# Fifteen small loads into an unread tile, issued behind the last row load of a sum of reciprocals

## The chip, the cores and the metric

The kernel runs on one core of a Trainium2 chip. The metric is device time in microseconds (us). A profile of one execution is at hand: its span runs from the first to the last instruction. In it PE is the matrix engine (PEld its weight loads), DVE the vector engine, ACT the activation engine, POOL the general engine, and SP the engine that issues all of this kernel's DMAs (SPq is its instruction queue).

## The reference

The input x is 32 x 512 x 1024 in float32, all positive. Each row of 1024 numbers gives one result, the sum of its reciprocals:

```python
def reference(x: np.ndarray) -> np.ndarray:
    return np.sum(1.0 / x, axis=-1).astype(np.float32)
```

## The kernel before

The 16384 rows are laid out as 128 partitions by F = 128 rows, so that a "row" of the kernel is 128 x 1024 numbers, 512 KB. A row is cut into two halves a and b. Because 1/a + 1/b = (a + b) / (a b), the kernel forms the product of the halves (POOL at L199, or DVE at L220 after PE has copied one half to PSUM at L209), takes its reciprocal on ACT as exp(-ln(.)) (L242 and L251), forms the sum of the halves on PE as two accumulating matmuls with the identity (L232) for some rows, and lets DVE multiply and sum along the row (L267) into one column of the tile `sums`. The last two rows, 126 and 127, are cut into two parts each, of 256 KB; so there are F + 2 = 130 work items.

The order of everything is written out by hand in the string PLAN (L38 to L73). Each token is an operation, an item number and perhaps a count and a bank: D loads the next so many items, P and V or W make products, C and S are matmuls, L and E the two activations, R the final reduction. The loop at L179 walks through the plan and issues the operations; each engine's queue keeps that order.

All DMAs are issued by SP, in this order:

- Loads (L187), into the tile `ring` of R = 40 row slots, so a later load must wait until the row that had its slot before has been used. There are 33 load instructions. The last four load 256 KB each: items 126 to 129. We number them load 1 to load 33.
- Six stores of finished columns of `sums` (L289), 19 columns each, which are put out when the first DONE = 114 rows have been reduced. We call them stores 1 to 6.
- One last store of the remaining 14 columns (L291), after the whole plan. We call it store 7.

The framework gives each DMA one of a small set of completion semaphores in turn, and puts the waits into the issuing queue. In the trace of this kernel, SP has one separate wait instruction at L187 for each of 25 of the 33 loads, and from load 9 on a DMA is issued only after the DMA eight places earlier has landed. So SP's queue is a chain with a stride of eight DMAs: load 33 behind load 25, store 1 behind load 26, and so on, besides the waits on compute engines. The function `note` (L135) records who touches which piece of the ring, a product slot or a bank, and declares some of the implied waits unnecessary. The direct stores at L289 and L291 are not passed to it.

After the body comes the end of the program (L317): SP waits for all DMAs, and the engines meet at barriers.

Of the kernel before, what the change touches and what calls it, by code (L numbers as in the profile page):

```python
# [11 lines left out]
def kernel(  # L12
# [5 lines left out]
    nc = tc.nc  # L18
    f32 = mybir.dt.float32
# [3 lines left out]
    F = 128  # L23
# [56 lines left out]
    x_v = x.flatten_outer_dims().rearrange("(p f) d -> p f d", p=P)  # L80
# [12 lines left out]
    pool = ctx.enter_context(tc.tile_pool(name="pool", bufs=1))  # L93
# [4 lines left out]
    prod = pool.tile([P, NP, H], f32)  # L98
    sums = pool.tile([P, F], f32)
    ident = pool.tile([P, P], f32)  # L100
    ps = pspool.tile([P, 8, H], f32)
    make_identity(nc, ident)

# [15 lines left out]
    def xs(r, h):  # L119
        q, at, w = place(r)  # L120
        return ring[:, q % R, at + h * w : at + (h + 1) * w]

    loaded = 0
# [54 lines left out]
    with tc.manual_schedule():  # L178
        for op, r, n, b in ops:  # L179
            p = pslot.get(r)  # L180
            if op == "D":
                n, r = r, loaded
                while n:
# [4 lines left out]
                        out=ring[:, a : a + m, at : at + 2 * w],  # L188
                        in_=x_v[:, q : q + m, at : at + 2 * w],
                    )  # L190
                    note("SP", inst, writes=rows(r, m))
                    r, n = r + m, n - m
                loaded = r
            elif op == "P":
                while n:
                    q, at, w = place(r)
# [3 lines left out]
                        out=prod[:, p : p + m, :w],  # L200
# [16 lines left out]
            elif op in "WV":  # L217
# [3 lines left out]
                    out=prod[:, p, :w], in0=xs(r, 0), in1=in1, op=mult  # L221
# [35 lines left out]
            elif op == "R":  # L257
# [4 lines left out]
                else:  # L262
# [5 lines left out]
                    out=row,  # L268
# [53 lines left out]
```

## Time and profile before

| what | value |
|---|---|
| time, median of 2 runs (168.21 and 168.22) | 168.22 us |
| span of the profiled execution | 166.3 us |
| granted PE clock, mean | 0.990 |
| PE busy | 132.5 us, 80% |
| DVE busy | 128.3 us, 77% |
| ACT busy | 132.3 us, 80% |
| POOL busy | 128.2 us, 77% |
| HBM read over the span | 67.11 MB, 404 GB/s |
| last load (load 33) issued | 153.51 us |
| store 7 issued | 164.06 us |

The profiled execution has no separate time on record; its span is 1.9 us less than the median of the runs, which is what lies before its first and after its last instruction. Every time of day below is counted from the start of that span. DMA issue is not counted as busy time in the profile, so SP does not appear among the engines of the first part; its instructions are found in the timeline and in the waits of SP.

### The profile page before, as it was taken

The numbers are of one execution on the slowest core, as the hardware profiler recorded it, in microseconds if no ns is written. First come the engines' busy times: TensorE is split into PE (matmuls) and PEld (weight loads), VectorE is DVE, ScalarE is ACT, GpSimd is POOL, SyncE is SP. The second block draws the span as 40 slices with busy tenths as digits, with TensorE's granted clock in tenths as the row PEclk, the third lists the DMA queues.
The fourth block names the chain that finished last, engine by engine and source line by source line (L and its number), as shares of the span: only waits on it lengthen the run. The fifth ranks groups of instructions, "written<-read, shape, count | busy, mean of one in ns | idle before, by whom it ended". The sixth has DMA issues, their size and how long they took to land.

```text
span 166.3 us, 1348 instructions
## 1 busy us (share of the span) xinstructions
PE 132.5 (80%) x292; PEld 55.2 (33%) x292; DVE 128.3 (77%) x282; ACT 132.3 (80%) x157; POOL 128.2 (77%) x81
## 2 busy tenths in 40 slices
PE   0000799978855999999999999988699979989982
PEld 0000333333312444444343433324234424433351
DVE  0000119885787699898998898989899999999994
ACT  3040073949995899999799999996999999999992
POOL 1500795069995999999999999948977869999860
PEclk9999999999996999999999999999999999999999
DMA  5999999999998989999999999999999999999940
GB/s 189 536 394 394 441 441 441 441 441 441 441 441 349 509 368 446 430 417 438 441 434 434 406 426 446 429 424 424 414 437 437 414 410 428 410 409 410 400 139 4
DMA packets 5768, 67.26 MB, mean 404 GB/s; under 512 B 1536, under 2 KB 1536, under 8 KB 3200
## 3 DMA queue, kind: packets, MB, share of 16 engines
q1 hardware_dynamic: 5760, 67.18, 95.6%
q8 instruction: 2, 0.03, 0.1%
q14 instruction: 6, 0.05, 0.1%
HBM read 67.11 MB, written 0.07 MB: 404 GB/s over the span
## 4 chain that ended last, share of the span: by engine, by line
DMA 57%; PE 18%; ACT 8%; DVE 6%; POOL 6%; issue 3%; SPq 1%; ACTq 0%; POOLq 0%; DVEq 0%
DMA ring<-in_x_dram 57%; PE ps L232 15%; POOL prod L199 6%; ACT prod L242 4%; PE ps L209 3%; ACT ps L251 2%; DVE ring L267 2%; DVE prod L267 2%; ACT prod L251 2%; DVE prod L220 1%; SPq L187 1%; DVE sums L267 0%; ACTq L242 0%; POOLq L199 0%; DVEq L317 0%
## 5 line engine op out<-in xcount | busy, mean ns | idle before, releaser
L199 POOL TENSOR_TENSOR prod<-ring 128x1024 f32<-128x1024 f32 (+2 forms) x75 | 127.5, 1727 | 33.5 <-DMA ring<-in_x_dram 27.1
L232 PE MATMUL ps<-ring,ident 128*128 128x512 f32 (+1 forms) x260 | 116.9, 596 | 5.2 <-DVE sums L267 4.5
L242 ACT ACTIVATE prod<-prod 128x1024 f32<-128x1024 f32 (+2 forms) x78 | 68.5, 892 | 24.9 <-DVE prod L220 14.3
L267 DVE CUSTOM_DVE_ANT_1 ring<-ring,ps 128x1024 f32<-128x1024 f32 (+1 forms) x65 | 76.4, 1208 | 8.9 <-ACT ps L251 8.7
L232 PEld LDWEIGHTS ps<-ring,ident 128*128 128x128 f32 x260 | 49.2, 193 | 71.7 <-issue 51.6
L267 DVE CUSTOM_DVE_ANT_0 prod<-prod,ps 128x512 f32<-128x512 f32 (+1 forms) x63 | 40.9, 677 | 0.4 <-PE ps L232 0.4
L209 PE MATMUL ps<-ring,ident 128*128 128x512 f32 x32 | 19.3, 689 | 25.7 <-DMA ring<-in_x_dram 24.0
L251 ACT ACTIVATE ps<-prod 128x1024 f32<-128x1024 f32 (+2 forms) x41 | 34.1, 838 | 4.5 <-DVE sums L267 3.7
L251 ACT ACTIVATE prod<-prod 128x1024 f32<-128x1024 f32 (+3 forms) x37 | 34.4, 931 | 0.9
L220 DVE TENSOR_TENSOR prod<-ring,ps 128x512 f32<-128x512 f32 x16 | 10.9, 684 | 26.3 <-PE ps L209 26.3
L209 PEld LDWEIGHTS ps<-ring,ident 128*128 128x128 f32 x32 | 6.0, 213 | 36.0 <-issue 21.4
L267 DVE DVE_READ_ACCUMULATOR2_ANT sums<- 128x1 f32 x130 | 10.7, 82 | 0.0
L220 DVE TENSOR_TENSOR prod<-ring 128x512 f32<-128x512 f32 x6 | 4.1, 688 | 0.1
L84 ACT ACT_TABLE_LOAD x1 | 1.3, 1283 | 0.7 <-PEq L306 0.7
L267 DVE CUSTOM_DVE_ANT_0 prod<-prod,ps,sums 128x256 f32<-128x256 f32 x2 | 0.9, 475 | 0.0
masks.py:197 POOL MEMSET ident<- 128x128 f32 x1 | 0.2, 204 | 0.3 <-POOLq L306 0.3
masks.py:199 POOL TENSOR_SCALAR_AFFINE_SELECT ident<-ident 128x128 f32<-128x128 f32 x1 | 0.3, 292 | 0.1
L306 POOL MEMSET const-float32-0.0<- 128x1 f32 x1 | 0.1, 98 | 0.2 <-issue 0.2
L306 POOL MEMSET const-bfloat16-1.0<- 128x1 bf16 x1 | 0.1, 101 | 0.0
L306 POOL MEMSET const-uint8-127<- 128x1 uint8 x1 | 0.1, 101 | 0.0
L306 POOL MEMSET const-float32-1.0<- 128x1 f32 x1 | 0.1, 98 | 0.0
## 6 DMA issues: line engine op xcount, KB each, us to landing
ring<-in_x_dram SPq DMA_DIRECT2D x2, 7168.0 KB, 41.2
ring<-in_x_dram SPq DMA_DIRECT2D x2, 3584.0 KB, 29.3
ring<-in_x_dram SPq DMA_DIRECT2D x2, 3072.0 KB, 31.9
ring<-in_x_dram SPq DMA_DIRECT2D x3, 2048.0 KB, 34.0
ring<-in_x_dram SPq DMA_DIRECT2D x1, 5632.0 KB, 30.3
ring<-in_x_dram SPq DMA_DIRECT2D x5, 1024.0 KB, 31.8
ring<-in_x_dram SPq DMA_DIRECT2D x1, 5120.0 KB, 16.5
ring<-in_x_dram SPq DMA_DIRECT2D x1, 4608.0 KB, 30.7
```

The lines of the kernel that those rows point to most:

```text
L84: nc.scalar.add_instruction(mybir.InstLoadActFuncSet(name=nc.get_next_instruction_name(), act_func_set_id=act_sets.index("natural_log_exp_ ...
L187: inst = nc.sync.dma_start(out=ring[:, a : a + m, at : at + 2 * w], in_=x_v[:, q : q + m, at : at + 2 * w],)
L199: inst = nc.gpsimd.tensor_tensor(out=prod[:, p : p + m, :w], in0=ring[:, a : a + m, at : at + w], in1=ring[:, a : a + m, at + w : at + 2 * w],
L209: inst = nc.tensor.matmul(ps[:, b, : place(r)[2]], lhsT=ident, rhs=xs(r, 1), start=True, stop=True,)
L220: inst = nc.vector.tensor_tensor(out=prod[:, p, :w], in0=xs(r, 0), in1=in1, op=mult)
L232: inst = nc.tensor.matmul(ps[:, b, : place(r)[2]], lhsT=ident, rhs=xs(r, h), start=h == 0, stop=h == 1,)
L242: inst = nc.scalar.activation(out=pg, in_=pg, func=Ln, scale=S)
L251: inst = nc.scalar.activation(out=rc, in_=pg, func=Exp, scale=-1.0)
L267: inst = nc.vector.tensor_tensor_reduce(out=row, in0=row, in1=other, scale=S, scalar=total if q in summed else 0.0, op0=mult, op1=add, acc ...
L306: nc = _bacc.Bacc("TRN2", target_bir_lowering=False, num_devices=1)
```

## The change

One more tile, `few`, of 16 x 136 float32 numbers is allocated after the others. When the last load has been issued, fifteen more loads follow it on SP: number k takes k + 1 numbers of each of k partitions from the input's first row into the columns of `few` that begin at k(k+1)/2. The column ranges of the fifteen don't overlap, each moves 4k(k+1) bytes (8 to 960), and nothing reads `few`. All else stays. In the queue of SP they stand behind load 33 and ahead of store 1. We call them tiny 1 to tiny 15.

```diff
     ident = pool.tile([P, P], f32)
+    few = pool.tile([16, 136], f32)
     ps = pspool.tile([P, 8, H], f32)
...
                 loaded = r
+                if loaded == F + 2:
+                    for k in range(1, 16):
+                        c = k * (k + 1) // 2
+                        nc.sync.dma_start(
+                            out=few[:k, c : c + k + 1], in_=x_v[:k, 0, c : c + k + 1]
+                        )
             elif op == "P":
```

## Prediction

> **What bounds the kernel now.** I read the page first, then the chain that ended last, then the waits of SP and SP's issues in the last 25 us, because the change touches only SP's queue.
>
> The page shows a kernel that is balanced on four engines and on DMA. Its strip of DMA use says when the loads stop:
>
> ```profile
> PE 132.5 (80%) x292; PEld 55.2 (33%) x292; DVE 128.3 (77%) x282; ACT 132.3 (80%) x157; POOL 128.2 (77%) x81
> DMA  5999999999998989999999999999999999999940
> ```
>
> The reader is to see that DMA is full until the slice that begins near 158 us (slices are 4.16 us) and free after 162: 4.4 us remain in which small transfers meet no traffic.
>
> The end of the chain of waits (start, us, what):
>
> ```profile
> 162.88 0.09 DVE prod L267
> 162.97 0.17 issue
> 163.14 0.08 DVE sums L267
> 163.23 0.18 DVE prod L267
> 163.40 0.14 issue
> 163.54 0.08 DVE sums L267
> 163.63 0.39 DVE prod L267
> 164.02 0.01 DVEq L317
> ```
>
> DVE sets the end: its last sum is ready at 164.03 and store 7 goes out at 164.06. The waits of SP over the whole span (who waited for whom: us in total, times, longest):
>
> ```profile
> SPq L187 <- DMA ring<-in_x_dram: 42.6, 16, 5.7
> SPq L289 <- DMA ring<-in_x_dram: 4.2, 6, 1.0
> SPq L291 <- DVE sums L267: 3.5, 1, 3.5
> SPq L291 <- DMA ring<-in_x_dram: 0.2, 1, 0.2
> ```
>
> All six stores wait for a load, though they read nothing that it writes: this is the stride of eight. The fourth line is the same for store 7, and the third is SP's slack: it stands idle 3.5 us until DVE is done. The issues of SP, from narrow windows of its timeline:
>
> ```profile
> 153.51 0.33 SPq L187 DMA_DIRECT2D ring<-in_x_dram  x1
> 154.80 0.35 SPq L289 DMA_DIRECT2D out_dram<-sums  x1
> 159.97 0.33 SPq L289 DMA_DIRECT2D out_dram<-sums  x1
> 164.06 0.33 SPq L291 DMA_DIRECT2D out_dram<-sums  x1
> ```
>
> Between them stores 2 to 5 went out at 156.08, 157.36, 158.69 and 159.36. The time from issue to landing, from the DMA view of the windows that hold loads 26 (issued 142.18), 33 and store 7, last column:
>
> ```profile
> ring<-in_x_dram SPq DMA_DIRECT2D x1, 512.0 KB, 12.6
> ring<-in_x_dram SPq DMA_DIRECT2D x1, 256.0 KB, 7.8
> out_dram<-sums SPq DMA_DIRECT2D x1, 7.0 KB, 1.4
> ```
>
> Load 26 lands at 142.18 + 12.6 = 154.78 and store 1 goes out at 154.80. Loads 27 to 32 land, by the same sum, at 156.07, 157.38, 158.69, 159.33, 159.86 and 160.54, and stores 2 to 6 follow them. Load 33 lands at 153.51 + 7.8 = 161.31.
>
> **The change part by part.** Nothing is removed. The unread tile costs no instruction. Fifteen DMA issues are put into SP's queue; what is queued behind them is stores 1 to 7 and SP's end of program, and no compute engine waits for those. Loads 1 to 33 stand ahead, so the compute chain up to 164.03 keeps its times. The bytes (4k(k+1) each, 5.4 KB in all) are nothing beside 67 MB, and stand behind the loads.
>
> 1. Tiny 1 to 7 take the places of the stores in the stride of eight: they wait for loads 26 to 32 and go out at 154.80, 156.08, 157.36, 158.69, 159.36, 159.97 and about 160.57. Cost nothing: the loads' landings 0.5 to 1.3 us apart cover an issue of about 0.4. Without that cover it would be an issue each, 7 x 0.4 = 2.8 us.
>
> 2. Tiny 8 waits for load 33: 161.31, issued about 161.33. Here the slack goes: where SP used to stand idle from 160.6, it now has 8 tiny and 6 stores ahead of store 7.
>
> 3. Tiny 9 to 15 wait for tiny 1 to 7. Store 1, issued at the same 154.80, landed 6.7 us later, at 161.5, as soon as the loads ahead of it were through; tiny 1 should be through by then too, so this costs at most 0.1 us, and the rest are bound by SP's own issue time. That price for a DMA of 1 to 15 partitions is not in the trace: all of its 40 have 128 partitions. Nearest rows: 29 isolated loads take 0.327 to 0.33, the first four, back to back, begin at 0.74, 1.17, 1.64 and 2.11, so 0.43 to 0.47 apart; the fourth takes 0.80 itself. From issue to issue that is 0.33 + 0.05 = 0.38 (the gap between the first loads is 0.05) at the low end, 0.43 to 0.47 in the back-to-back rows, and 0.85 at the worst. Nothing says that a small DMA must be dearer or cheaper to issue. I take 0.425, the middle between the isolated and the dearest normal row, since these are back to back but have few pieces: 8 x 0.425 = 3.40, so store 1 goes out at 161.33 + 3.40 = 164.73.
>
> 4. Stores 1 to 6: six issues at 0.38 (the row 0.332 to 0.348 and the gap) = 2.28, and about 0.05 for each of three separate semaphore waits, which stand ahead of stores 5 to 7 (17 ns and a gap each) = 0.15. Their landing waits are old: store 1 needs tiny 8, issued 3.4 us before, where store 7 landed after 1.4 and store 6, behind loads, after 2.4. Store 7 goes out at 164.73 + 2.28 + 0.15 = 167.16 instead of 164.06.
>
> 5. After store 7 all stays: 1.4 us to landing, then the barriers to 166.31. By then stores 1 to 6 would land at their own 1.4 after issue, ahead of store 7.
>
> Sum: 167.16 - 164.06 = 3.10 us, so a span of 169.4. The profiled span of 166.3 stands 1.9 under the median of 168.22, and that part isn't touched: 168.22 + 3.10 = **171.3 us**, 1.8% more.
>
> Ends of the unknown: at 0.327 for each of the 14 issues, with no gap, 161.33 + 4.58 + 0.15 = 166.06, 2.0 us more, 170.2. At 0.70 per tiny, toward the dear row of 0.80, 161.33 + 5.60 + 2.43 = 169.36, 5.3 us more, 173.5. At 0.85, tiny 5 to 8 would slip too (159.36 + 3 x 0.85 = 161.91), and store 7 would go out at 171.1, 7.1 us more: 175.3.
>
> Against the middle price stands a rule of the Trainium skill, page "DMA: Bandwidth & Descriptors", section "Why a DMA increments its semaphore by 16 and not by 1": a transfer is spread over the largest number of engines up to 16 that divides its outermost size, and where that is below 16 the issuing sequencer itself writes the missing part of the semaphore count. All the tiny loads are such, and no row here shows one; the page gives no price for it on this chip. By it alone the issue would be dearer than 0.38, and each 0.1 us more would add 0.8.
>
> The row of the final store gives 1.4 us to landing, and stores 1 to 6 landed 161.5 to 162.4, a few tenths apart, so their latencies overlap. The same page, section "Anatomy of one DMA — SWDGE (gpsimd) path", gives about 2.0 us fixed per DMA, on another path. Paid one after another for fifteen that would be an estimate of 30 us more, 198; paid under the stride of eight, tiny 8 would land at an estimated 163.3 and the sum stays 171.3. The rows speak for the second.
>
> **The rivals.**
>
> *Slower by over 2%: the tiny issue is dear.* The place is SP between 161.33 and store 1. All other terms kept, the 2% line (171.58, 3.36 us more) is crossed at 3.40 + 0.26 = 3.66 for eight, 0.458 us each. For it: two of the three back-to-back rows are 0.47, and 0.47 gives 171.7; 0.60 gives 172.7. Against: 29 rows of 0.33, and the first loads were of 1 to 7 MB, with many more pieces.
>
> *Hidden.* If the tiny loads had no lane wait, SP could issue all from 153.84 on, be through at 153.84 + 15 x 0.425 = 160.2, and issue the six stores by 162.6, before DVE is done: 168.22. Against: stores wait for loads that they have nothing to do with, six times. With the waits but almost no issue time, store 1 would still wait for tiny 8 to land, 161.33 + 1.4 = 162.7, and store 7 go out at 165.2: 169.3.
>
> *Serial.* If the framework took the fifteen writes into one tile for overlapping, each would wait for the one before to land: tiny 2 at about 161.4, tiny 15 after 13 x 1.4 more at 179.6, the stores at 0.4 each, store 7 at 182.4, 18.4 us more, 186.6. Against: the first four loads write one tile too and go out 0.43 to 0.47 apart, and the columns are disjoint.
>
> *Faster.* No mechanism: DVE's end at 164.03 is ahead of the change in no queue.
>
> **How the numbers follow.** The forecast, a tiny interval between about 0.33 and 0.458, has 0.52. Dear issue has 0.41, as two of the three nearest rows lie on that side of the line. Hidden or nearly free 0.04, serial 0.02, faster 0.01. A measurement of this kernel can tell about 2% from no change. Slower by over 2% is dear and serial: 0.43. Same is forecast and hidden: 0.56. Faster 0.01. The range from 170.2 to 173.5 leaves out hidden and faster below (0.05), the serial case and the dear ones over 0.70 (some 0.10).
>
> **What would show it.** In the profile after: the loads and all compute at their old times up to 164.0; SP's tiny 1 to 7 at the stores' old places from 154.8; tiny 8 at the landing of load 33 near 161.3; tiny 8 to 15 one after another, 0.38 to 0.47 apart; SP's wait on DVE at L291 gone; the chain of waits ending in SP's issues rather than in DVE; store 7 at 167.2. I am wrong if a tiny's issue takes clearly another time than 0.33 to 0.42, if tiny 9 stands long behind tiny 1's landing, or if stores 1 to 6 wait for tiny landings.

## The result, and the profile after

The changed kernel takes 172.04 us (171.91 and 172.17) against 168.22: a ratio of 1.0226, with a 95% interval of 1.0207 to 1.0244, 3.8 us more. The forecast was 171.3 and within 2%; the time lies inside the range of 170.2 to 173.5 and just over the line. The span grew from 166.3 to 170.1, the same 3.8.

The end of the chain of waits, after (start, us, what):

```profile
163.56 0.08 DVE sums L274
163.65 0.39 DVE prod L274
164.04 0.01 DVEq L324
```

It is the old chain, 0.02 us later: no compute engine noticed the change. This view follows the engines and stops at 164.04, although the span goes on to 170.1; the last six microseconds have to be read elsewhere. The waits of SP, after:

```profile
SPq L198 <- DMA ring<-in_x_dram: 5.4, 8, 1.1
SPq L324 <- DMA out_dram<-sums: 0.6, 1, 0.6
```

Eight of the tiny loads (L198) wait for loads 26 to 33, in the places that the stores had. The two lines of the last store, with SP's 3.5 us of idle time, are gone, and no store waits for anything. The issues of SP after load 32's landing, from narrow windows of its timeline (start, us):

```profile
160.61 0.27 SPq L198 DMA_DIRECT2D few<-in_x_dram  x1
161.25 0.27 SPq L198 DMA_DIRECT2D few<-in_x_dram  x1
161.57 0.29 SPq L198 DMA_DIRECT2D few<-in_x_dram  x1
...
163.02 0.60 SPq L198 DMA_DIRECT2D few<-in_x_dram  x1
163.67 0.37 SPq L198 DMA_DIRECT2D few<-in_x_dram  x1
164.09 0.37 SPq L198 DMA_DIRECT2D few<-in_x_dram  x1
164.51 0.38 SPq L296 DMA_DIRECT2D out_dram<-sums  x1
164.93 0.43 SPq L296 DMA_DIRECT2D out_dram<-sums  x1
165.41 0.43 SPq L296 DMA_DIRECT2D out_dram<-sums  x1
165.88 0.43 SPq L296 DMA_DIRECT2D out_dram<-sums  x1
166.81 0.33 SPq L296 DMA_DIRECT2D out_dram<-sums  x1
167.25 0.36 SPq L296 DMA_DIRECT2D out_dram<-sums  x1
167.72 0.44 SPq L298 DMA_DIRECT2D out_dram<-sums  x1
```

Tiny 8 goes out at 161.25, when load 33 has landed; from there SP works without a wait until store 7 goes out at 167.72, 3.66 us after its old 164.06. Three things meet the eye: the issue time grows with the number of partitions (behind another issue, 0.29 for 9 and 0.37 for 15); tiny 13, at 163.02, takes 0.60; and between the end of store 4 at 166.31 and store 5 at 166.81 there is a hole of 0.50 us. In 0.43 of that SP does nothing that the trace shows; the rest is a separate wait instruction for tiny 12, whose last semaphore event had come at 164.57, long before.

### The profile page after: what moved, and what is told of

Same layout as the page of the kernel before. It is cut to its first block, busy times and chain, and to the rows that moved or that the text cites. A ratio compares the mean times of both kernels' runs of the same rounds, so it can differ in the third digit from the quotient of the medians.

```text
span 170.1 us, 1363 instructions
## 1 busy us (share of the span) xinstructions
PE 132.7 (78%) x292; PEld 55.3 (33%) x292; DVE 128.2 (75%) x282; ACT 132.3 (78%) x157; POOL 128.2 (75%) x81
## 4 chain that ended last, share of the span: by engine, by line
DMA 56%; POOL 31%; issue 3%; ACT 2%; DVE 2%; PE 1%; SPq 1%; POOLq 0%; DVEq 0%
DMA ring<-in_x_dram 56%; POOL prod L206 31%; ACT prod L249 1%; DVE ring L274 1%; PE ps L239 1%; DVE prod L274 1%; SPq L188 1%; ACT prod L258 1%; ACT ps L258 1%; DVE prod L227 0%; DVE sums L274 0%; POOLq L206 0%; DVEq L324 0%
```

## The experiments

Theory Q (queue): the loss is the SP issues that stand between the landing of load 33 and store 7. Rivals: a price for each added DMA wherever it stands (A), and small DMAs that land late and hold the stores (L). The edits are against the changed kernel unless they say otherwise. Ratios are to the kernel before on the same chip; the loss is the ratio minus 1, times 168.1. "Stretch" is read from the profiles: from the first issue behind load 33's landing to the issue of store 7. In the kernel before it is 164.06 - 161.31 = 2.75 us, nearly all of it idle.

| kernel | ratio (95%) | loss, us | stretch, us | stretch - 2.75 |
|---|---|---|---|---|
| the change | 1.0226 (1.0207 to 1.0244) | 3.8 | 6.47 | 3.72 |
| tiny 1 to 6 alone | 1.0053 (1.0035 to 1.0072) | 0.9 | 2.83 | 0.08 |
| reversed order | 1.0190 (1.0172 to 1.0208) | 3.2 | 5.78 | 3.03 |
| behind the six stores | 1.0214 (1.0183 to 1.0245) | 3.6 | 6.03 | 3.28 |
| one store for six | 1.0077 (1.0056 to 1.0097) | 1.3 | 3.94 | 1.19 |
| one partition each | 1.0175 (1.0158 to 1.0192) | 2.9 | 5.55 | 2.80 |
| 128 partitions each | 1.0289 (1.0270 to 1.0308) | 4.9 | 7.12 | 4.37 |
| before, fifteen stores | 1.0130 (1.0114 to 1.0147) | 2.2 | 4.30 | 1.55 |
| thirty tiny loads | 1.0557 (1.0541 to 1.0573) | 9.4 | 12.18 | 9.43 |

The last column gives the loss within 0.5 us in every row but the second and the eighth, which are taken up below.

**Tiny 1 to 6 alone.**

```diff
-                    for k in range(1, 16):
+                    for k in range(1, 7):
```

> Only tiny 1 to 6. Theory Q (queue): what costs is the number and kind of SP issues that stand between the landing of load 33 (161.25) and store 7; the issue time is paid there and nowhere else. Here tiny 1 to 6 take the six places behind loads 26 to 31, store 1 goes out behind load 32 at 160.6, store 2 behind load 33 at 161.25 to 161.3, store 6 four issues of 0.43 to 0.54 later at 163.0 to 163.4, and store 7 is ready for 164.06, when DVE is done: 168.2, at most 168.5. Rival A (each added DMA has its price wherever it stands, 3.82 / 15 = 0.25 us): 168.22 + 6 x 0.25 = 169.7. Rival L (the stores behind are held by the late landing of small DMAs): store 7 waits for store 1 to 6 and their places only, about 169.

Measured 168.93 against 167.99. The numbers of theory Q and of rival A were wrong. Rival L's "about 169" is what was measured, but not for its reason: no store waits for a tiny load in the waits of SP, and store 7 was issued when DVE was done, as theory Q has it. So the queue was free; but the end came late. The lines of SP's drains at the end of the program (shortest, median, longest ns; first and last start):

```profile
L324 SPq DRAIN  x3: 7/7/7, 166.3 to 166.6; - x3
```

From store 7 (164.26) to the first drain it takes 2.0 us, where the kernel before takes 165.54 - 164.06 = 1.5. Counting issues and separate waits, the hole of some 0.43 us that the changed kernel has behind store 4 now lies there, behind a wait of the program's end. In both it stands behind SP's 19th instruction after load 33. This opened a second question, taken up with the last four kernels.

**Reversed order.**

```diff
-                    for k in range(1, 16):
+                    for k in range(15, 0, -1):
```

> The same fifteen, from 15 partitions down to 1. Theory Q with a price by partitions (0.24 to 0.27 us for 2 to 8 partitions and 0.29 to 0.37 for 9 to 15, as the profile of the changed kernel shows, each with a gap of 0.045): the eight behind load 33 have 8 to 1 partitions, 2.46 instead of 3.26 us: 171.2. Theory Q with a price set by the pace of back-to-back issues, whatever their size: 172.0. Rival A: 172.0.

Measured 171.26, 0.6 us less lost than in the change. The eight behind load 33 now have 8 to 1 partitions and take 163.68 - 161.11 = 2.57 us instead of 3.26. Not all of that is the partitions: the reversed run has no long issue such as that of tiny 13, which took 0.60 where its neighbours took 0.34 and 0.37, so about 0.25 of the 0.69 is that and 0.45 the price by partitions. A price for each DMA (A) would have kept 172.0.

**Behind the six stores.**

```diff
-                if loaded == F + 2:
-                    for k in range(1, 16):
...
+        for k in range(1, 16):
...
         nc.sync.dma_start(out=out_v[:, DONE:], in_=sums[:, DONE:])
```

> The fifteen stand between store 6 and store 7 instead of ahead of store 1. Theory Q: stores 1 to 6 keep their old places, tiny 1 goes out behind load 32 at 160.6, tiny 2 to 15 from 161.3 on; by the issue times of the changed kernel they take 4.8 to 5.1 us with a price by partitions, 5.7 at 0.41 each, so store 7 goes out at 166.1 to 167.0: 170.3 to 171.2, less than the changed kernel because six stores are no longer behind load 33. Rival A: 172.0, as the number of DMAs is the same.

Measured 171.68 (171.27 to 172.16), above what theory Q gave, and its interval holds the change's ratio, so the time tells the theories apart no better than that. In its profile load 33 is issued 0.2 to 0.5 us later than in the other eight kernels of the table, which no edit explains; the stretch is 6.03, shorter than 6.47 but longer than my 4.8 to 5.7. Two stops of about 0.4 us (one of them the hole that is taken up below) and two long issues (0.50 and 0.56) are in it. I count this run as inconclusive.

**One store for six.**

```diff
-                    for c in range(0, DONE, DONE // 6):
-                        part = slice(c, min(c + DONE // 6, DONE))
+                    for c in range(0, DONE, DONE):
+                        part = slice(c, min(c + DONE, DONE))
```

> The tiny loads as in the change, and one store of 114 columns in place of the six of 19. Theory Q: tiny 8 to 15 as before the same 3.26 us, store 1 at 164.5, store 7 one issue later at 165.0 instead of 167.7: 169.2 to 169.5, so the six stores carry 2.7 us of the loss of the changed kernel. Rival A: fifteen tiny loads at 0.25, 172.0, less 1.25 if five missing stores give back as much each: 170.8. Rival L: store 7 no earlier than the landing of tiny 9, which is over by then, so the same as Q here.

Measured 169.37, inside theory Q's range and 1.4 under rival A's. Store 7 goes out 165.31 - 164.83 = 0.48 after the one store. So 2.5 of the 3.8 us are five of the old stores, which the tiny loads pushed out of the time in which SP waited, with the hole of 0.43 that stood among them; it now lies behind store 7, where SP waits for the last landing anyway.

**One partition each, and 128 partitions each.**

```diff
-                            out=few[:k, c : c + k + 1], in_=x_v[:k, 0, c : c + k + 1]
+                            out=few[:1, c : c + k + 1], in_=x_v[:1, 0, c : c + k + 1]
```

> The fifteen loads have one partition each, with the same 2 to 16 numbers. Theory Q with a price by partitions: eight issues behind load 33 at 0.24 to 0.30 us and a gap of 0.045, 2.3 to 2.8 instead of 3.26 us: 171.1 to 171.6. Theory Q with a pace of back-to-back issues that does not go by partitions: 172.0. Rival A: 172.0.

```diff
-    few = pool.tile([16, 136], f32)
+    few = pool.tile([P, 136], f32)
...
-                            out=few[:k, c : c + k + 1], in_=x_v[:k, 0, c : c + k + 1]
+                            out=few[:, c : c + k + 1], in_=x_v[:, 0, c : c + k + 1]
```

> The fifteen loads have 128 partitions each, with the same 2 to 16 numbers. Theory Q: eight issues behind load 33 at the pace of the stores of the changed kernel (3.21 us for six, 0.535 each), 4.3 instead of 3.26 us: 173.1; if the pace is 0.41 whatever the size: 172.0. Rival L (few partitions, so that few engines carry the transfer, make it land late and hold the stores): faster than 172.0, as all engines carry these.

Measured 171.00 and 172.87, before 168.10: theory Q by partitions both times, and against rival L, by which the wide ones should have been faster. From the timeline, tiny 8, the first behind load 33, tiny 9 or 15, and store 1; first with one partition:

```profile
161.22 0.22 SPq L198 DMA_DIRECT2D few<-in_x_dram  x1
163.28 0.24 SPq L198 DMA_DIRECT2D few<-in_x_dram  x1
163.56 0.38 SPq L296 DMA_DIRECT2D out_dram<-sums  x1
```

then with 128:

```profile
161.32 0.33 SPq L198 DMA_DIRECT2D few<-in_x_dram  x1
161.70 0.43 SPq L198 DMA_DIRECT2D few<-in_x_dram  x1
165.17 0.43 SPq L296 DMA_DIRECT2D out_dram<-sums  x1
```

Eight issues take 2.34 us with one partition (0.29 each) and 3.85 with 128 (0.48 each, one long issue of 0.58 among them). A 128-partition DMA takes 0.33 after a pause and 0.43 behind another one, whether it loads 40 bytes a partition or stores 76; where a separate wait instruction stands between the two, it takes 0.35 to 0.38.

**The kernel before, with fifteen stores.**

```diff
-                    for c in range(0, DONE, DONE // 6):
-                        part = slice(c, min(c + DONE // 6, DONE))
+                    for c in range(0, DONE, 8):
+                        part = slice(c, min(c + 8, DONE))
```

> The kernel before, without tiny loads; the first 114 columns leave in fifteen stores of 8 (the last of 2) instead of six of 19. Theory Q: store 8 goes out behind load 33 at 161.3, seven more and then the last store of 14 columns, eight issues at 0.47 to 0.535: the last at 165.1 to 165.6 instead of 164.06: 169.2 to 169.8. A rival that puts the loss on something that only small loads do (few engines, an unread tile, small writes into the on-chip memory): 168.2.

Measured 170.28, without any tiny load: the loss is not a property of small loads or of an unread tile, it is the number of issues behind load 33. My size was too low by 0.5 to 1.1. The last store goes out at 165.70:

```profile
161.40 0.33 SPq L289 DMA_DIRECT2D out_dram<-sums  x1
161.78 0.43 SPq L289 DMA_DIRECT2D out_dram<-sums  x1
...
164.82 0.38 SPq L289 DMA_DIRECT2D out_dram<-sums  x1
165.70 0.33 SPq L291 DMA_DIRECT2D out_dram<-sums  x1
```

That is 0.1 above the range for the issue, and 1.64 us later than in the kernel before; the hole is here again, behind the store at 164.82. The other 0.5 us of the loss came after it: SP waited at the program's end until 167.6 for a landing, 1.9 us after the last issue, where the kernel before needs 1.4. Why it lands later was not tried.

**Thirty tiny loads.**

```diff
-    few = pool.tile([16, 136], f32)
+    few = pool.tile([16, 272], f32)
...
-                    for k in range(1, 16):
-                        c = k * (k + 1) // 2
+                    for n in range(30):
+                        k = n % 15 + 1
+                        c = k * (k + 1) // 2 + n // 15 * 136
```

> Thirty tiny loads, the fifteen twice over into other columns. Theory Q: fifteen more issues behind load 33; at 0.35 each (the mean of the issue times in the changed kernel and the gap) 5.3 us more, at 0.45 (with a stall now and then) 6.7 more: 177.3 to 178.8. Rival A: 168.22 + 30 x 0.25 = 175.9.

Measured 177.50: theory Q, and 1.6 above rival A. The second fifteen cost 5.6 us, the first 3.8, as the first had SP's slack to use up.

**The hole.** In the change and in all eight the hole, 0.42 to 0.44 us, stands behind the 19th of SP's instructions after load 33 that the trace shows, whichever it is: behind store 4 in the change, behind a tiny load in the run with thirty, behind store 15 in the run with fifteen stores. Counted from the start, it is the 79th, separate waits included (of these, in the kernel before, 25 stand ahead of 21 of the loads). In the kernel before, the 79th is the last drain (165.85), where the gap to the next is 0.44, against 0.38 in the changed kernel, whose hole is elsewhere: it was there all along, hidden in the last barrier. Four kernels move it, by empty instructions put into SP's queue behind load 4, where SP is idle:

```diff
                 loaded = r
+                if loaded == R:
+                    for _ in range(13):
+                        nc.sync.drain()
```

The first has them in the changed kernel, the second three and the third ten in the kernel before, the fourth thirteen together with tiny 1 to 6 alone.

> The changed kernel with thirteen empty instructions (drains without a wait) put into SP's queue behind load 4, where SP stands idle for 32 us. In the changed kernel and in the eight experiments so far SP stands still for 0.42 to 0.44 us behind its 19th instruction after load 33, whichever that is. Theory B (boundary: the stop belongs to a place in SP's instruction stream, counted from its start): it moves to behind tiny 6, where SP waits for a load anyway, and the changed kernel loses 0.4 us less: 171.6, with store 5 following store 4 without a gap. Rival P (the stop comes from a pressure of four stores issued back to back): unchanged, 172.0, and the gap stays between stores 4 and 5.

> The kernel before with three empty instructions behind load 4. Theory B: the stop, which lies before at the very end behind the 19th instruction, where the last barrier takes 0.38 us anyway, moves three instructions up, to behind the first drain after the last landing, where nothing covers it: 0.35 to 0.43 us more, 168.6. Rival P: 168.2, unchanged.

> The kernel before with ten empty instructions behind load 4. Theory B: the stop moves into the time in which SP waits for DVE ahead of store 7: 168.15 to 168.2, the same or 0.06 less. If the empty instructions themselves cost something at the end, 168.3 or more.

> Tiny 1 to 6 alone, with thirteen empty instructions behind load 4. With tiny 1 to 6 alone store 7 kept its place but the end came 0.9 us later; its profile has the stop of 0.43 us between the last landings and the barriers. Theories Q and B together: with the stop moved ahead of store 1 the six tiny loads cost nothing, 168.2 to 168.4. Rival A (0.15 us for each added DMA, by that run): still 169.1.

Measured: 171.45, ratio 1.0198 (1.0175 to 1.0221); 168.50, 1.0021 (1.0009 to 1.0034); 168.23, 1.0000 (0.9986 to 1.0014); 168.31, 1.0002 (0.9986 to 1.0018). All four go with theory B, and rival P is out in the second, whose stores are not changed at all. The first one's interval overlaps that of the change, so there the profile carries it. Stores 4, 5 and 6 and store 7 of that kernel:

```profile
165.79 0.43 SPq L299 DMA_DIRECT2D out_dram<-sums  x1
166.32 0.37 SPq L299 DMA_DIRECT2D out_dram<-sums  x1
166.79 0.38 SPq L299 DMA_DIRECT2D out_dram<-sums  x1
167.26 0.38 SPq L301 DMA_DIRECT2D out_dram<-sums  x1
```

The hole between stores 4 and 5 is closed (166.22 to 166.32), and store 7 is 0.46 earlier. In the second kernel the drains of SP show where three instructions have put it; first the kernel before, then the second:

```profile
L317 SPq DRAIN  x3: 7/7/7, 165.5 to 165.9; - x3
L320 SPq DRAIN  x3: 7/7/116, 165.7 to 166.5; - x3
```

From the first to the last drain it takes 0.8 us instead of 0.3 (165.54 to 165.85). And in the fourth the first drain is back at 1.6 us after store 7 (164.09):

```profile
L327 SPq DRAIN  x3: 7/7/7, 165.7 to 166.0; - x3
```

So six tiny loads cost nothing that these runs can tell from zero once the hole lies in idle time. Of the 0.9 us of the first experiment its profile puts 0.43 down to the hole and 0.1 to two more waits at the program's end; another 0.2 stand ahead of load 33, where nothing was edited, and are not explained. No version was faster than the kernel before.

## Why the prediction was right, and where it was off

The place and the mechanism were right: tiny 1 to 7 took the stores' places at no cost (154.83 to 160.61); tiny 8 left with load 33's landing; the slack of 3.5 us was used up; the compute chain stayed; and store 7 became late by an amount that is a sum of issue times and one stop. The side of the 2% line was missed: the larger chance, 0.56, stood on a loss within 2%, and the interval of 1.0207 to 1.0244 lies wholly above. By terms:

- Tiny 8: predicted 161.33, came at 161.25: -0.08.
- Eight tiny issues: 3.40, came to 3.26: -0.14. Right in sum and wrong in kind: I took 0.425 for each. They cost 0.32 (8 partitions, issue to issue) to 0.42 (15 partitions), and one of 0.65 fills it up. That the sum came out is luck, and the prediction's own sign of being wrong, an issue clearly outside 0.33 to 0.42, came true at both ends: tiny 8 took 0.27 and tiny 13 took 0.60.
- **Six stores and three waits: 2.43, came to 3.21: +0.78. This is the step that failed**, step 4, "six issues at 0.38". Two things are in it: the hole, 0.43, of which the profile of before shows no sign that could be read as such, and 0.35 from the pace. I priced the tiny loads with the back-to-back rows of the first loads (0.43 to 0.47) and the stores with the isolated row (0.33). It is the other way round: the stores have 128 partitions and stand back to back, so the rows of the first loads were theirs.
- After store 7: 0, came to 0.16 (2.41 us to the end instead of 2.25).

The sum is 0.72 over 171.32 (168.22 + 3.10), which is 172.04. Without the hole ahead of store 7, as in the first of the last four kernels, the ratio is 1.0198 (1.0175 to 1.0221), and the side is not clear. The rival "dear issue" named the right side of the 2% line with the wrong cause: the tiny issues were not dear. The serial and the hidden rival fell: no tiny load waited for the one before it, and the stride of eight held. That the chain of waits would end in SP's issues was a misreading of what that view follows.

The rule from the Trainium skill, page "DMA: Bandwidth & Descriptors", section "Why a DMA increments its semaphore by 16 and not by 1", by which few partitions mean few engines and an extra write by the sequencer, agrees with the trace. The fifteen loads have 240 packets, two for each partition, as if each of k engines moved one piece and posted one completion. And the semaphore events show one more than k: tiny 8, with 8 partitions, raises its semaphore nine times, once at 161.69 and eight times from 162.42 to 162.49, where each store raises it sixteen times. Who writes the ninth the trace does not say.

```profile
q1 hardware_dynamic: 6000, 67.18, 93.5%
```

(The kernel before has 5760 on that queue.) I took the rule as speaking for a dearer issue. The measurement decides otherwise: after a pause, 0.22 for one partition, 0.27 for 8, 0.33 for 128.

What stays open: what the hole is. It belongs to a fixed place in SP's instruction stream: three empty instructions move it by three, and with ten and thirteen it is gone from its old place and would lie in a wait. One thing in the traces goes with it. In each of the eleven kernels in which its end can be read, a packet of 8192 bytes on the instruction queue q14 begins 0.6 to 0.9 us after that end (in the change at 167.41, behind 166.74), and in the three others such a packet comes early too, between 161.3 and 161.9. So the hole may have to do with the supply of instructions; that is not shown. Also open is the long issue of tiny 13 (below).

## What to carry to other kernels

A queue that looks idle at the end may be the one that sets it as soon as something is put ahead of its last instruction: count the issues between the last event that the queue has to wait for and its last store, and set their sum against the slack. Price each issue by its own kind, by its width and by whether it stands behind another. What is put into a stride of waits takes the places of what was there, and the displaced work is what costs: here 2.5 of 3.8 us were the old stores and the stop among them.

## What the runs showed of the hardware that was not expected

- SP stands still for 0.42 to 0.44 us at one place in its instruction stream. Three empty instructions, issued some 160 us earlier, made the kernel before 0.2% slower by moving it; ten did not.
- A DMA's issue time on SP goes with its partitions, but only while they are few. After a pause it is 0.22 us for 1, 0.27 for 8, 0.33 for 14 (reversed order) and 0.33 for 128 (the first of the fifteen is longer, 0.30 for 1); behind another issue it is 0.25, 0.37 and 0.43 for 1, 15 and 128. So 128 partitions cost no more than 14 after a pause. A price by the engines that a DMA is spread over, as many as the partitions up to 15 by the packets and 16 for 128, would fit this better than one by the partitions; no run tells the two apart.
- Single issues take longer without a wait, 0.60 for tiny 13. The DMA view of the window 163.02 to 163.62 has a packet of another queue in it:

```profile
q14 instruction: 1, 0.01, 4.6%
q1 hardware_dynamic: 36, 0.00, 3.2%
```

  The runs with 128 partitions (0.73 for store 7) and with thirty loads (0.70 for one of seven partitions) have such a packet in their long issues too. In all the kernels together, each of the eleven issues behind load 33 that took 0.50 us or more overlaps one; but other issues beside such a packet are not long, among them all of those with one partition. That it is the cause was not tried.
